# Normalising inside the turn: products with a diagonal instead of transposes, scale and shift on ScalarE, in a hybrid decoder layer

## The chip, the cores and the metric

The kernel runs on one core of a Trainium2 chip. The metric is the device time of one execution in microseconds (us). Five engines work beside each other, each through its own queue in order: TensorE (PE in the profile) multiplies matrices from SBUF into PSUM, VectorE (DVE), ScalarE (ACT) and GpSimd (POOL) work on elements, and SyncE (SP) issues the DMAs.

## The reference, cut to what matters

One layer over x of 512 tokens by 2048 channels, float32: a norm with modulation from the conditioning vector c, a mixing block of sixteen heads (HGRN2 and gated delta rule), a second norm with modulation, and a squared-ReLU MLP of 8192 channels.

```python
def rmsnorm(x, w):
    y = x * lax.rsqrt(jnp.mean(x * x, axis=-1, keepdims=True) + EPS)
    return y * w
mod = silu(c) @ w_ada + b_ada
sh_m, sc_m, gt_m, sh_f, sc_f, gt_f = jnp.split(mod, 6)
h = rmsnorm(x, pre_mix_norm) * (1.0 + sc_m) + sh_m
proj = h @ w_in
y = concatenate([hgrn2_group(proj), gdn_group(proj)]) @ w_out
x = x + gt_m * rmsnorm(y, post_mix_norm)
h = rmsnorm(x, pre_ffn_norm) * (1.0 + sc_f) + sh_f
y = jnp.square(jax.nn.relu(h @ w_ff1)) @ w_ff2
return x + gt_f * rmsnorm(y, post_ffn_norm)
```

The two lines that begin with `h =` are what the change touches. The mean over channels gives one reciprocal root per token; scale and shift are one number per channel.

## The kernel before, in words

Products with large weights want the activations with channels on the partitions, and x arrives with tokens on them. So each of the 16 slices of 128 channels (`kt`) is turned: four blocks of 128 tokens by 128 channels go through TensorE into one PSUM bank of 128 x 512. Every large product is done in a split form: a float32 value is cut into a high part `H` (type float32r) and the rest `L`, and `mm3` adds three products, H by H, H by L and L by H. Weights are split on the way by `WeightStream._split`: ScalarE casts (`wh`, line 197), VectorE or, for some, GpSimd subtracts (`wl`, line 199).

**The start stage.** `ada_thread` (line 786) loads w_ada in slots and adds up the modulation sums `asum`: the scale half on VectorE (line 440), the shift half by ScalarE and GpSimd (lines 449 and 451) from the second slice on. `x_thread` (line 618) squares x on ScalarE as it arrives, gets the reciprocal root of each token block with `rsqrt_to` (VectorE, then a power on GpSimd), multiplies the identity by it (`dgx`, line 641), and spreads it over all partitions by a product of ones with that diagonal (`prx`) and a copy into R1 (line 626). `mod_thread` (line 826) takes the slices one group after the other (0, 1, then pairs). For each it sums the modulation over partitions on TensorE (`pc`), forms the columns `sc1` and `shm` on VectorE, turns the slice (`x_transposes`, line 822, into the bank `wh`, of which there is one; slice 0 is turned early, into `sg`), and then:

- VectorE multiplies the turned slice by the column `sc1` and by R1 into `ht` (line 858);
- for slices below 4 and odd ones, ScalarE adds the shift into `hH` (line 862), and VectorE makes `hL` (line 863);
- for the other six, ScalarE adds the shift into `ht` (line 866) and casts it to `hH` (line 867), and GpSimd subtracts (line 868).

The start products (`start_unit`, line 665; sixteen output blocks of two heads) use each slice as soon as it is there: partial sums leave PSUM by line 703 (ScalarE, first time) or 705 (VectorE, added).

The order on TensorE, ScalarE and SyncE in this stage is the order in which the program issues, and that is set by `run` (line 876): it holds an estimate of TensorE's time (`clock`, advanced by `mm` and `tp` by a fixed cost for each product), lets the thread that is due by that clock go on, and otherwise issues the next start product from the fill thread. VectorE and GpSimd are ordered by the framework. Fill that is not issued in the stage goes on in the mixing stage behind it.

**The middle.** After the output product `pout` (line 1495) the rows z, still with tokens on partitions, get the first norm and the residual (`residual`, line 1464), their reciprocal root again (`rsm`), a diagonal `dg` and its spread into R (`pre_norm`, line 1477), and are stored to DRAM (line 1483). From line 1516 the 16 slices are transposed (`pm`) through four PSUM banks in turn, VectorE applies scale and R (`h2t`, line 1525), and the split follows: for two of three slices by ScalarE and VectorE (lines 1528 and 1529), for the third by two ScalarE passes and GpSimd (lines 1533 to 1535). `ff1` (line 1562) uses the slices at once (`pf`). Here the framework orders the transposes among the `pf` products.

Of the kernel before, what the change touches and what calls it, by code (L numbers as in the profile page):

```python
# [8 lines left out]
F32 = mybir.dt.float32  # L9
# [3 lines left out]
AF = mybir.ActivationFunctionType  # L13
ALU = mybir.AluOpType

P = 128
# [17 lines left out]
T = 512  # L34
# [201 lines left out]
def hybrid_layer_kernel(  # L236
# [7 lines left out]
    nc = tc.nc  # L244
# [80 lines left out]
    def bank(tag, name):  # L325
        return psx.tile([P, T], F32, tag=tag, name=name, bufs={"pj": PJ, "wg": 5 - PJ}.get(tag, 1))
# [3 lines left out]
    def mm(ps, lhsT, rhs, start=True, stop=True, cost=None):  # L330
        nc.tensor.matmul(ps, lhsT=lhsT, rhs=rhs, start=start, stop=stop)  # L331
        n = 1
        for k in rhs.shape[1:]:
            n *= k
        if rhs.dtype == F32R:
            clock[0] += max(n, 256) / 512 * 0.2135
        else:
            m = lhsT.shape[1]
            clock[0] += max(n, m) / 512 * 0.87 if cost is None else cost

    def tp(ps, in_):
        nc.tensor.transpose(out=ps, in_=in_, identity=ident)
        clock[0] += 0.107
# [6 lines left out]
    ident = const.tile([P, P], F32, name="ident")  # L350
    make_identity(nc, ident)
    ones = const.tile([P, P], F32, name="ones")
# [54 lines left out]
    sc1 = const.tile([P, KT], F32, name="sc1")  # L407
# [203 lines left out]
    junk = sp.tile([P, 1024], BF16, name="junkx")  # L611
    rstd = sp.tile([P, 4], F32, name="rstdx")
    stage = sp.tile([P, 4, T], F32, name="stage")
    R1 = sp.tile([P, T], F32, name="R1")
    xn = [xn4[:, tok, :] for tok in range(4)]
    early = {}

    def x_thread():
        yield "xload", 0
        early[0] = bank("sg", "pt0")  # L620
        pr = bank("sh", "prx")

        def spread(tok, dg):
            ts = slice(tok * P, (tok + 1) * P)
            mm(pr[:, ts], ones, dg)
            nc.vector.tensor_copy(out=R1[:, ts], in_=pr[:, ts])

        for tok in range(4):
            for hf in range(2):
                yield max(0.0, xarr[2 * tok + hf] + 1.0 - clock[0])  # L630
                if hf == 0:
                    tp(early[0][:, tok * P : (tok + 1) * P], xn[tok][:, :P])
                nc.scalar.activation(out=junk, in_=xn4[:, tok, hf * 1024 : (hf + 1) * 1024], func=AF.Square,
                                     accum_out=ssx2[:, hf, tok : tok + 1])
                if hf == 0 and tok > 0:
                    spread(tok - 1, dg)
            nc.vector.tensor_tensor(out=ssx[:, tok : tok + 1], in0=ssx2[:, 0, tok : tok + 1],
                                    in1=ssx2[:, 1, tok : tok + 1], op=ALU.add)
            rsqrt_to(rstd[:, tok : tok + 1], ssx[:, tok : tok + 1], 1.0 / D, EPS)
            dg = sp.tile([P, P], F32, tag="dgx", bufs=2, name=f"dgx{tok}")  # L640
            nc.vector.tensor_scalar(out=dg, in0=ident, scalar1=rstd[:, tok : tok + 1], scalar2=None, op0=ALU.mult)
        ws._split()
        yield 2.5
        spread(3, dg)
        yield 0.35
        tokens.add(("x", 0))

# [173 lines left out]

    def x_transposes(ps, kt):
        for tok in range(4):
            tp(ps[:, tok * P : (tok + 1) * P], xn[tok][:, kt * P : (kt + 1) * P])

    def mod_thread():
        for g, kts in enumerate(GROUPS):
            w = len(kts) * P
            if g > 0:
                next(masking, None)  # L830
            if g == 3:
                late_consts()
            yield "ada", g
            yield 2.0 if g else 0.5
            n = len(kts)
            asc, ash = sums.pop(g)
            pc = sm(f"pc{g}").rearrange("p (k n) -> p k n", n=64)
            nr = 1 if g < NV else 512 // w
            for i in range(n):
                column_sum(pc, i, asc[:, i * P : (i + 1) * P], ones[:, :64])  # L840
                for r in range(nr):
                    column_sum(pc, n + i, ash[:, r * w + i * P : r * w + (i + 1) * P], ones[:, :64],
                               r == 0, r == nr - 1)
            ks = slice(kts[0], kts[0] + n)
            nc.vector.tensor_tensor(out=sc1[:, ks], in0=pc[:, 0:n, 0], in1=b_scm[:, ks], op=ALU.add)
            nc.vector.tensor_tensor(out=sc1[:, ks], in0=sc1[:, ks], in1=w_pm[:, ks], op=ALU.mult)
            nc.vector.tensor_tensor(out=shm[:, ks], in0=pc[:, n : 2 * n, 0], in1=b_shm[:, ks], op=ALU.add)
            if g == 0:
                yield "x", 0
            for kt in kts:  # L850
                if kt in early:
                    ps = early[kt]
                else:
                    yield 0.5
                    ps = sm(f"pt{kt}")
                    x_transposes(ps, kt)
                ht = mt("ht", f"ht{kt}", 2)
                nc.vector.scalar_tensor_tensor(out=ht, in0=ps, scalar=sc1[:, kt : kt + 1], in1=R1,
                                               op0=ALU.mult, op1=ALU.mult)
                yield 0.0  # L860
                if kt < 4 or kt % 2:
                    nc.scalar.activation(out=hH[:, kt, :], in_=ht, func=AF.Identity, bias=shm[:, kt : kt + 1])
                    nc.vector.scalar_tensor_tensor(out=hL[:, kt, :], in0=ht, scalar=shm[:, kt : kt + 1],
                                                   in1=hH[:, kt, :].bitcast(F32), op0=ALU.add, op1=ALU.subtract)
                else:
                    nc.scalar.activation(out=ht, in_=ht, func=AF.Identity, bias=shm[:, kt : kt + 1])
                    nc.scalar.copy(out=hH[:, kt, :], in_=ht)
                    nc.gpsimd.tensor_tensor(out=hL[:, kt, :], in0=ht, in1=hH[:, kt, :].bitcast(F32),
                                            op=ALU.subtract)
                yield 1.0  # L870
                tokens.add(("mod", kt))
        yield from decay_terms()
# [572 lines left out]
    with ExitStack() as st:  # L1445
# [4 lines left out]
        ssm = mp.tile([P, 2, 4], F32, name="ssm")  # L1450
        rsm = mp.tile([P, 2, 4], F32, name="rsm")
        junk = mp.tile([P, 1024], BF16, name="junkm")
        R = mp.tile([P, T], F32, name="R")

        def scaled(ps, tok, nb):
            nc.scalar.activation(out=junk[:, :512], in_=ps, func=AF.Square, accum_out=ssy[:, tok, nb : nb + 1])
# [18 lines left out]
            rsqrt_to(rsm[:, 1, tok : tok + 1], ssm[:, 1, tok : tok + 1], 1.0 / D, EPS)  # L1475

        def pre_norm(tok):
            dg = mp.tile([P, P], F32, tag="dg", name=f"dg{tok}", bufs=2)
            nc.vector.tensor_scalar(out=dg, in0=ident, scalar1=rsm[:, 1, tok : tok + 1], scalar2=None, op0=ALU.mult)
            pr = bank("wh", f"pr{tok}")  # L1480
            nc.tensor.matmul(pr[:, :P], lhsT=ones, rhs=dg, start=True, stop=True)
            nc.vector.tensor_copy(out=R[:, tok * P : (tok + 1) * P], in_=pr[:, :P])
            nc.sync.dma_start(out=x2d[tok * P : (tok + 1) * P, :], in_=z[:, tok, :])

        for tok in range(3):
# [30 lines left out]
        for kt in range(KT):  # L1516
            ps = bank(("wg", "wg", "sh", "sg")[kt % 4], f"pm{kt}")
            for tok in range(4):
                nc.tensor.transpose(out=ps[:, tok * P : (tok + 1) * P], in_=z[:, tok, kt * P : (kt + 1) * P],
                                    identity=ident)  # L1520
            if kt == 0:
                h2H = big.tile([P, KT, T], F32R, tag="hH", name="h2H")
                h2L = big.tile([P, KT, T], F32R, tag="hL", name="h2L")
            ht = mp.tile([P, T], F32, tag="ht2", bufs=2, name=f"h2t{kt}")
            nc.vector.scalar_tensor_tensor(out=ht, in0=ps, scalar=sc1f[:, kt : kt + 1], in1=R,
                                           op0=ALU.mult, op1=ALU.mult)
            if kt % 3 < 2:
                nc.scalar.activation(out=h2H[:, kt, :], in_=ht, func=AF.Identity, bias=shf[:, kt : kt + 1])
                nc.vector.scalar_tensor_tensor(out=h2L[:, kt, :], in0=ht, scalar=shf[:, kt : kt + 1],
                                               in1=h2H[:, kt, :].bitcast(F32), op0=ALU.add, op1=ALU.subtract)  # L1530
            else:
                hs = mp.tile([P, T], F32, tag="h2s", bufs=1, name=f"h2s{kt}")
                nc.scalar.activation(out=hs, in_=ht, func=AF.Identity, bias=shf[:, kt : kt + 1])
                nc.scalar.copy(out=h2H[:, kt, :], in_=hs)
                nc.gpsimd.tensor_tensor(out=h2L[:, kt, :], in0=hs, in1=h2H[:, kt, :].bitcast(F32),
                                        op=ALU.subtract)

    partst.close()

# [264 lines left out]
```

## Time and profile before

| | |
|---|---|
| median of 3 runs | 2586.42 us (2584.91 to 2587.82) |
| the profiled execution, its own time | 2583.66 us |
| its span in the trace | 2581.9 us |
| granted TensorE clock, mean | 0.986 |
| TensorE busy | 2469.1 us, 96% |
| VectorE busy | 1875.9 us, 73% |
| ScalarE busy | 1118.1 us, 43% |
| GpSimd busy | 1032.4 us, 40% |

How to read it. The profile is of one execution. Its rows name the line of the kernel, the engine, the operation and the tiles (out <- in), then a count and durations; "L331 PE MATMUL pt<-..." is a product issued by the helper at line 331 into the tile pt. A float32 product shows as two instructions, a transpose as one. Matmul durations overlap, so what a product costs in a stream is the distance between starts. Idle time is put down to what ended it: "<-DVE ht L858" means that VectorE's `ht` came last. The granted clock is TensorE's, as a share of full speed.

### The profile page before, as it was taken

To read this page: it belongs to the slowest core of one execution; us is meant where nothing else is said; L and a number is where in the kernel's file an instruction comes from. 1 tells how busy PE (TensorE), PEld (TensorE's weight loads), DVE (VectorE), ACT (ScalarE), POOL (GpSimd) and SP (SyncE) were. 2 spreads that over 40 slices of the span, in tenths; PEclk is the share of its full clock that TensorE was granted. 3 is DMA by queue.
4 is the path that set the end of the run, shared out by engine and by line. 5 is a ranking of instruction groups with operands and counts; after the bars stand their busy time and mean duration, and the time that the engine had idled before them with its cause. 6 is when DMAs were issued, how large, how long until landed. Compare 5 with 4: busy or idle time off the path is not lost.

```text
span 2581.9 us, 34110 instructions
## 1 busy us (share of the span) xinstructions
PE 2469.1 (96%) x12627; PEld 2007.2 (78%) x12627; DVE 1875.9 (73%) x2709; ACT 1118.1 (43%) x1765; POOL 1032.4 (40%) x646
## 2 busy tenths in 40 slices
PE   5889999998999899999999999999999999999998
PEld 3667777777777778788788888888888888888876
DVE  7997877768586765634668776777768777677787
ACT  5553544544444452423444444444434434443333
POOL 5561344445444440000244535445354444533333
PEclk9999999999999999999999999999999999999999
DMA  8762434444545432344423332433424333232334
GB/s 320 255 203 74 128 119 147 139 148 138 160 142 164 139 115 82 130 140 155 154 98 133 104 135 95 146 123 106 142 95 139 110 127 135 94 114 82 122 116 161
DMA packets 127300, 350.64 MB, mean 136 GB/s; under 512 B 14247, under 2 KB 18713, under 8 KB 125981
## 3 DMA queue, kind: packets, MB, share of 16 engines
q1 hardware_dynamic: 126938, 348.41, 40.0%
q8 instruction: 99, 1.62, 0.3%
q14 instruction: 67, 0.55, 0.1%
q10 hardware_dynamic: 196, 0.06, 0.0%
HBM read 340.01 MB, written 8.40 MB: 135 GB/s over the span
## 4 chain that ended last, share of the span: by engine, by line
PE 67%; DVE 6%; POOL 1%; ACT 1%; issue 1%; DMA 1%; DVEq 0%; ACTq 0%; POOLq 0%
PE pf L331 27%; PE pg L331 22%; PE pj L331 9%; PE pout L331 7%; DVE wl L199 1%; DVE uc L1034 1%; PE pa L331 1%; DVE utmp L1032 1%; POOL y L1728 0%; POOL aacc L451 0%; PE p L331 0%; DVE x2r L1746 0%; DMA ada<-in_w_ada_dram 0%; DVE zkT L493 0%; PE pz L331 0%
## 5 line engine op out<-in xcount | busy, mean ns | idle before, releaser
L199 DVE TENSOR_TENSOR wl<-raw,wh 128x1024 fp32r<-128x1024 f32 x506 | 720.1, 1424 | 427.8 <-ACT wh L197 422.6
L197 ACT CAST wh<-raw 128x1024 fp32r<-128x1024 f32 x512 | 538.0, 1052 | 943.4 <-PE pf L331 285.9
L165 POOL TENSOR_TENSOR raw<-raw,raw 128x1024 f32<-128x1024 f32 x150 | 438.9, 2941 | 392.7 <-DMA raw<-in_w_ff_dram 181.6
L331 PE MATMUL pf<-h2L,wh 128*128 128x512 f32 x1024 | 399.9, 391 | 0.0
L331 PE MATMUL pf<-h2H,wh 128*128 128x512 f32 x1024 | 399.7, 390 | 0.0
L331 PE MATMUL pf<-h2H,wl 128*128 128x512 f32 x1024 | 399.6, 390 | 0.0
L451 POOL TENSOR_TENSOR aacc<-ada,aacc 128x512 f32<-128x512 f32 x180 | 268.9, 1494 | 253.5 <-ACT ada L449 242.2
L331 PE MATMUL pg<-wl,cH 128*128 128x512 f32 x840 | 327.6, 390 | 1.1 <-DVE wl L199 1.1
L331 PE MATMUL pg<-wh,cL 128*128 128x512 f32 x840 | 327.3, 390 | 0.0
L331 PE MATMUL pg<-wh,cH 128*128 128x512 f32 x840 | 327.3, 390 | 0.0
L331 PE MATMUL pj<-hH,wh 128*128 128x512 f32 x768 | 325.2, 423 | 0.0
L331 PE MATMUL pj<-hH,wl 128*128 128x512 f32 x768 | 305.0, 397 | 4.4 <-DVE wl L199 4.4
L331 PE MATMUL pj<-hL,wh 128*128 128x512 f32 x768 | 304.0, 396 | 0.0
L331 PEld LDWEIGHTS pf<-h2H,wh 128*128 128x128 f32 x1024 | 192.7, 188 | 39.7
L331 PEld LDWEIGHTS pf<-h2L,wh 128*128 128x128 f32 x1024 | 192.7, 188 | 39.6
L331 PEld LDWEIGHTS pf<-h2H,wl 128*128 128x128 f32 x1024 | 192.7, 188 | 39.6
L451 POOL TENSOR_TENSOR gacc<-ada,gacc 128x512 f32<-128x512 f32 x64 | 108.4, 1694 | 278.9 <-ACT ada L449 278.9
L1627 DVE TENSOR_TENSOR y<-pg,y 128x512 f32<-128x512 f32 x344 | 219.0, 682 | 0.0
L331 PEld LDWEIGHTS pg<-wl,cH 128*128 128x128 f32 x840 | 157.8, 188 | 35.0 <-DVE wl L199 2.3
L331 PEld LDWEIGHTS pg<-wh,cH 128*128 128x128 f32 x840 | 157.8, 188 | 32.7
L331 PEld LDWEIGHTS pg<-wh,cL 128*128 128x128 f32 x840 | 157.8, 188 | 32.5
L331 PEld LDWEIGHTS pj<-hH,wl 128*128 128x128 f32 x768 | 146.4, 191 | 39.2 <-DVE wl L199 6.5
(434 smaller groups left out, 3770.3 us busy)
## 6 DMA issues: line engine op xcount, KB each, us to landing
raw<-in_w_ff_dram SPq DMA_DIRECT2D x256, 512.0 KB, 4.0
raw<-in_w_in_dram SPq DMA_DIRECT2D x128, 512.0 KB, 3.4
ada<-in_w_ada_dram SPq DMA_DIRECT2D x256, 256.0 KB, 3.4
adas<-in_w_ada_dram SPq DMA_DIRECT2D x128, 256.0 KB, 4.4
raw<-in_w_out_dram SPq DMA_DIRECT2D x40, 512.0 KB, 3.5
xo<-in_x_dram SPq DMA_DIRECT2D x8, 512.0 KB, 9.4
xr<-in_x_dram SPq DMA_DIRECT2D x8, 512.0 KB, 6.8
x2d<-z SPq DMA_DIRECT2D x4, 1024.0 KB, 5.7
```

The source lines that it names most:

```text
L165: self.nc.gpsimd.tensor_tensor(out=out, in0=ra, in1=rb, op=op)
L197: self.cast = self.nc.scalar.copy(out=h, in_=raw).ins
L199: eng.tensor_tensor(out=lo, in0=raw, in1=h.bitcast(F32), op=ALU.subtract)
L331: nc.tensor.matmul(ps, lhsT=lhsT, rhs=rhs, start=start, stop=stop)
L451: nc.gpsimd.tensor_tensor(out=acc, in0=a, in1=acc, op=ALU.add)
L1032: nc.vector.tensor_tensor(out=tmp[:, :, :n], in0=xj, in1=uc[:, :, j : j + 1].broadcast_to([P, NCH, n]), op=ALU.mult)
L1034: nc.vector.tensor_tensor(out=uc[:, :, j + 1 :], in0=uc[:, :, j + 1 :], in1=tmp[:, :, :n], op=ALU.subtract)
L1627: nc.vector.tensor_tensor(out=dst, in0=ps, in1=dst, op=ALU.add)
```

## The change

At both norms the reciprocal root is no longer spread over partitions and multiplied in by VectorE. The turn itself does it: the block of x or z is multiplied by the diagonal `dg` of its tokens' roots instead of by the identity, as an ordinary float32 product. The copies R1 and R, and the products that filled them, go; the four diagonals of each norm are kept. Scale and shift are then applied by ScalarE in one activation from PSUM, twice for each slice in the start stage: once into `hH` and once, in full float32, into `ht`, and `hL` is the difference. In the middle the second, full one (`hs`) is made by VectorE from PSUM for even slices and by ScalarE for odd ones; GpSimd subtracts for every fourth slice, VectorE for the others.

```diff
     def x_thread():
         yield "xload", 0
         early[0] = bank("sg", "pt0")
-        pr = bank("sh", "prx")
-
-        def spread(tok, dg):
-            ts = slice(tok * P, (tok + 1) * P)
-            mm(pr[:, ts], ones, dg)
-            nc.vector.tensor_copy(out=R1[:, ts], in_=pr[:, ts])
...
+    def turn(ps, tok, kt):
+
+        mm(ps[:, tok * P : (tok + 1) * P], xn[tok][:, kt * P : (kt + 1) * P], dgs[tok])
...
                 if hf == 0 and tok > 0:
-                    spread(tok - 1, dg)
+                    turn(early[0], tok - 1, 0)
...
                 ht = mt("ht", f"ht{kt}", 2)
-                nc.vector.scalar_tensor_tensor(out=ht, in0=ps, scalar=sc1[:, kt : kt + 1], in1=R1,
-                                               op0=ALU.mult, op1=ALU.mult)
+                sb = dict(scale=sc1[:, kt : kt + 1], bias=shm[:, kt : kt + 1])
+                nc.scalar.activation(out=hH[:, kt, :], in_=ps, func=AF.Identity, **sb)
+                nc.scalar.activation(out=ht, in_=ps, func=AF.Identity, **sb)
                 yield 0.0
-                if kt < 4 or kt % 2:
-                    nc.scalar.activation(out=hH[:, kt, :], in_=ht, func=AF.Identity, bias=shm[:, kt : kt + 1])
-                    nc.vector.scalar_tensor_tensor(out=hL[:, kt, :], in0=ht, scalar=shm[:, kt : kt + 1],
-                                                   in1=hH[:, kt, :].bitcast(F32), op0=ALU.add, op1=ALU.subtract)
-                else:
-                    nc.scalar.activation(out=ht, in_=ht, func=AF.Identity, bias=shm[:, kt : kt + 1])
-                    nc.scalar.copy(out=hH[:, kt, :], in_=ht)
-                    nc.gpsimd.tensor_tensor(out=hL[:, kt, :], in0=ht, in1=hH[:, kt, :].bitcast(F32),
-                                            op=ALU.subtract)
+                eng = nc.vector if kt < 4 or kt % 2 else nc.gpsimd
+                eng.tensor_tensor(out=hL[:, kt, :], in0=ht, in1=hH[:, kt, :].bitcast(F32), op=ALU.subtract)
                 yield 1.0
...
-            pr = bank("wh", f"pr{tok}")
-            nc.tensor.matmul(pr[:, :P], lhsT=ones, rhs=dg, start=True, stop=True)
-            nc.vector.tensor_copy(out=R[:, tok * P : (tok + 1) * P], in_=pr[:, :P])
+            dg2.append(dg)
...
-                nc.tensor.transpose(out=ps[:, tok * P : (tok + 1) * P], in_=z[:, tok, kt * P : (kt + 1) * P],
-                                    identity=ident)
+                nc.tensor.matmul(ps[:, tok * P : (tok + 1) * P], lhsT=z[:, tok, kt * P : (kt + 1) * P],
+                                 rhs=dg2[tok], start=True, stop=True)
...
+            hs = mp.tile([P, T], F32, tag="h2s", bufs=3, name=f"h2s{kt}")
+            sb = dict(scale=sc1f[:, kt : kt + 1], bias=shf[:, kt : kt + 1])
+            nc.scalar.activation(out=h2H[:, kt, :], in_=ps, func=AF.Identity, **sb)
+            if kt % 2 == 0:
+                nc.vector.tensor_scalar(out=hs, in0=ps, scalar1=sb["scale"], scalar2=sb["bias"],
+                                        op0=ALU.mult, op1=ALU.add)
             else:
...
+                nc.scalar.activation(out=hs, in_=ps, func=AF.Identity, **sb)
+            eng = nc.gpsimd if kt % 4 == 3 else nc.vector
+            eng.tensor_tensor(out=h2L[:, kt, :], in0=hs, in1=h2H[:, kt, :].bitcast(F32), op=ALU.subtract)
```

The early transposes of slice 0 in `x_thread` go too (its turn takes their place), `dgx` and `dg` get four buffers instead of two, and the `ht2` tiles of the middle go.

More of the change, by code (lines that the diff above doesn't have):

```diff
@@ L613, in hybrid_layer_kernel @@
     stage = sp.tile([P, 4, T], F32, name="stage")
-    R1 = sp.tile([P, T], F32, name="R1")
+    dgs = []
     xn = [xn4[:, tok, :] for tok in range(4)]
     early = {}
+    def turn(ps, tok, kt):
+        mm(ps[:, tok * P : (tok + 1) * P], xn[tok][:, kt * P : (kt + 1) * P], dgs[tok])
     def x_thread():
@@ L630, in x_thread @@
                 yield max(0.0, xarr[2 * tok + hf] + 1.0 - clock[0])
-                if hf == 0:
-                    tp(early[0][:, tok * P : (tok + 1) * P], xn[tok][:, :P])
                 nc.scalar.activation(out=junk, in_=xn4[:, tok, hf * 1024 : (hf + 1) * 1024], func=AF.Square,
@@ L639, in x_thread @@
             rsqrt_to(rstd[:, tok : tok + 1], ssx[:, tok : tok + 1], 1.0 / D, EPS)
-            dg = sp.tile([P, P], F32, tag="dgx", bufs=2, name=f"dgx{tok}")
+            dg = sp.tile([P, P], F32, tag="dgx", bufs=4, name=f"dgx{tok}")
             nc.vector.tensor_scalar(out=dg, in0=ident, scalar1=rstd[:, tok : tok + 1], scalar2=None, op0=ALU.mult)
+            dgs.append(dg)
         ws._split()
         yield 2.5
-        spread(3, dg)
+        turn(early[0], 3, 0)
         yield 0.35
@@ L823, in x_transposes @@
         for tok in range(4):
-            tp(ps[:, tok * P : (tok + 1) * P], xn[tok][:, kt * P : (kt + 1) * P])
+            turn(ps, tok, kt)
     def mod_thread():
@@ L1452, in hybrid_layer_kernel @@
         junk = mp.tile([P, 1024], BF16, name="junkm")
-        R = mp.tile([P, T], F32, name="R")
+        dg2 = []
         def scaled(ps, tok, nb):
@@ L1477, in pre_norm @@
         def pre_norm(tok):
-            dg = mp.tile([P, P], F32, tag="dg", name=f"dg{tok}", bufs=2)
+            dg = mp.tile([P, P], F32, tag="dg", name=f"dg{tok}", bufs=4)
             nc.vector.tensor_scalar(out=dg, in0=ident, scalar1=rsm[:, 1, tok : tok + 1], scalar2=None, op0=ALU.mult)
-            pr = bank("wh", f"pr{tok}")
-            nc.tensor.matmul(pr[:, :P], lhsT=ones, rhs=dg, start=True, stop=True)
-            nc.vector.tensor_copy(out=R[:, tok * P : (tok + 1) * P], in_=pr[:, :P])
+            dg2.append(dg)
             nc.sync.dma_start(out=x2d[tok * P : (tok + 1) * P, :], in_=z[:, tok, :])
@@ L1523, in hybrid_layer_kernel @@
                 h2L = big.tile([P, KT, T], F32R, tag="hL", name="h2L")
[L1524 to L1530, printed above, removed]
-            else:
[L1532 to L1536, printed above, removed]
+            hs = mp.tile([P, T], F32, tag="h2s", bufs=3, name=f"h2s{kt}")
[4 more added lines that the diff above has]
+                                        op0=ALU.mult, op1=ALU.add)
+            else:
+                nc.scalar.activation(out=hs, in_=ps, func=AF.Identity, **sb)
+            eng = nc.gpsimd if kt % 4 == 3 else nc.vector
+            eng.tensor_tensor(out=h2L[:, kt, :], in0=hs, in1=h2H[:, kt, :].bitcast(F32), op=ALU.subtract)
     partst.close()
```

## The prediction

> **What bounds the kernel now.** I read the page first, then busy times by stretch, who waited for whom, the tiles that the change touches, and the order of time around line 1516.
>
> ```profile
> span 2581.9 us, 34110 instructions
> PE 2469.1 (96%) x12627; PEld 2007.2 (78%) x12627; DVE 1875.9 (73%) x2709; ACT 1118.1 (43%) x1765; POOL 1032.4 (40%) x646
> PE   5889999998999899999999999999999999999998
> ```
>
> TensorE sets the time: it is busy for 96% of the span, and after the first slices (64.5 us each) nearly always. What adds TensorE work adds time, unless it lands where TensorE now waits. So I look for its gaps, where the change works.
>
> ```profile
> 27.43:60.00 32.57, 24.75 (x110) 18.91 (x112) 30.28 (x46) 19.15 (x43) 14.32 (x10) 0.84 0.85 299
> 60.00:90.00 30.00, 25.53 (x149) 19.73 (x144) 27.15 (x42) 17.94 (x38) 16.37 (x11) 0.94 0.82 298
> 90.00:120.00 30.00, 21.27 (x108) 15.80 (x109) 29.35 (x41) 12.34 (x24) 18.57 (x13) 0.96 0.66 224
> 120.00:150.00 30.00, 26.91 (x125) 20.92 (x124) 26.92 (x36) 15.81 (x31) 18.49 (x13) 0.87 0.75 249
> 150.00:180.00 30.00, 24.94 (x142) 19.37 (x141) 28.30 (x42) 12.58 (x24) 15.13 (x10) 0.89 0.74 237
> 180.00:205.00 25.00, 24.08 (x130) 17.55 (x130) 19.95 (x20) 11.70 (x21) 14.30 (x9) 1.00 0.22 69
> 205.00:230.00 25.00, 25.00 (x117) 19.50 (x116) 12.26 (x21) 12.71 (x24) 3.16 (x5) 1.00 0.21 69
> 1235.50:1246.00 10.50, 4.42 (x28) 3.33 (x26) 6.46 (x15) 3.84 (x8) 1.15 (x3) 0.75 0.44 181
> 1246.00:1270.00 24.00, 24.00 (x119) 19.97 (x118) 21.85 (x27) 15.02 (x23) 6.57 (x5) 0.90 0.10 26
> ```
>
> The columns are the stretch, its length, the busy time of TensorE (PE), its weight loads, VectorE (DVE), ScalarE (ACT) and GpSimd (POOL), then granted clock and DMA. Between 27.43 and 205 TensorE is idle for 7.8 + 4.5 + 8.7 + 3.1 + 5.1 + 0.9 = 30.1 us. VectorE is the full engine there: 111.72 of the 120 us from 60 to 180. From 205 TensorE is full. In the middle it is idle for some 6 us before 1246, then full while the second norm's slices are made.
>
> ```profile
> PE pc L331 <- DVE asum L440: 10.3, 4, 5.9
> PE pt L342 <- DVE shm L847: 4.7, 4, 2.0
> PE pph L331 <- DVE parth L705: 3.7, 1, 3.7
> ...
> ACT ht L866 <- DVE ht L858: 35.6, 6, 9.7
> ACT hH L862 <- DVE ht L858: 16.1, 7, 8.6
> ```
>
> Total wait, times, longest. TensorE waits for VectorE, and ScalarE stood for 51.7 us behind `ht`, the very pass that goes.
>
> **Start stage, the product.** A transpose of a 512-wide slice is four TensorE instructions; a product with a float32 diagonal shows two instructions for each 128x128 block.
>
> ```profile
> 1228.43 0.22 PE pr L1481 x2
> ...
> 1242.87 0.30 DVE dg L1479
> ...
> 1243.21 0.81 PE pr L1481 x2
> ...
> 1244.04 0.30 DVE R L1482
> ...
> 1244.37 0.76 DVE h2t L1525
> ...
> 1254.30 0.44 PE pm L1519 x4
> ```
>
> At full clock one such product, `pr`, advanced TensorE by 0.22 us; four transposes took 0.44. Four products take 4 x 0.22 = 0.88, so a slice costs 0.44 more. Slice 0's blocks and the removed `prx` products lie before 27.43, in idle time. The other fifteen: 15 x 0.44 = +6.6 us. Does the 30 us of idle time hide it? Start products still run long after the stage:
>
> ```profile
> L331 PE MATMUL pph<-hH,wh x112: 388/390/797, 48.8 to 292.1; 128*128 128x512 f32 x112
> ```
>
> `run` (line 876) fills TensorE's order with such products whenever no thread is due on its own clock, and `mm` puts 0.87 us on that clock for a slice where `tp` put 0.43. The longer turn therefore pushes fill out of the stage, to behind 205, where TensorE is full. I count all 6.6 us; what can shrink is the idle time, by itself:
>
> ```profile
> L858 DVE SCALAR_TENSOR_TENSOR ht<-pt,sc,R x16: 739/750/753, 25.9 to 199.6; 128x512 f32<-128x512 f32 x16
> L862 ACT ACTIVATE hH<-ht,shm x10: 706/722/726, 26.7 to 200.4; 128x512 fp32r<-128x512 f32 x10
> L863 DVE SCALAR_TENSOR_TENSOR hL<-ht,shm,hH x10: 744/956/2876, 28.3 to 201.1; 128x512 fp32r<-128x512 f32 x10
> L866 ACT ACTIVATE ht<-ht,shm x6: 722/724/727, 84.0 to 197.9; 128x512 f32<-128x512 f32 x6
> L867 ACT CAST hH<-ht x6: 617/621/624, 84.7 to 198.7; 128x512 fp32r<-128x512 f32 x6
> ...
> L626 DVE COPY R<-prx x4: 292/292/292, 18.1 to 25.5; 128x128 f32<-128x128 f32 x4
> ...
> L705 DVE TENSOR_TENSOR parth<-pph,parth x15: 677/682/692, 78.8 to 232.2; 128x512 f32<-128x512 f32 x15
> ```
>
> **Start stage, VectorE.** It loses 16 x 0.75 = 12.0 us of `ht`, the last copy of R (0.29; the others ran while it waited), and on ten `hL` the difference between 0.744 and a plain subtract, by the nearest row 0.68: 0.6. Together 12.9 us, the upper bound of what the idle time can lose through VectorE. The lower bound is zero, for this reason: `ht` reads PSUM and is never stretched (739 to 753 ns), but `hL`, both inputs in SBUF, went from 744 to 2876. The sums that fill VectorE do the same:
>
> ```profile
> L440 DVE SCALAR_TENSOR_TENSOR asum<-adas,c,asum 128x256 f32<-128x256 f32 x105 | 88.4, 842 | 2.0
> ...
> 152.05 1.00 DVE L440 SCALAR_TENSOR_TENSOR asum<-adas,c,asum 128x256 f32<-128x256 f32 x2
> ```
>
> Two took 1.00 us when undisturbed, so 0.50 each, against a mean of 0.84. GpSimd is busy for 68.6 of the 120 us between 60 and 180, 57%. Freed VectorE time that falls under a GpSimd operation may only become waiting: spread evenly, 43% of 12.9 = 5.5 us would be kept. More was clear of GpSimd, because ScalarE, which feeds it, stood behind `ht`; with that wait gone GpSimd's work will spread over VectorE's. I take 8, between 5.5 and 12.9 and nearer to 5.5.
>
> The Trainium skill, page "SBUF — State Buffer", section "Who interferes with whom", says that a VectorE instruction with two SBUF inputs contends with a GpSimd instruction that reads SBUF, and one with a single SBUF input does not. The trace agrees in those two rows (753 ns at most against 2876). Taken to its end the rule speaks against this change: it takes away only VectorE work that never contended. That is the first rival below.
>
> **Start stage, ScalarE.** Two activations per slice from PSUM with a scale and a bias column replace one of 0.72 (ten slices) or 0.72 + 0.62 (six): 15.3 us now. No row has both columns. Bounds: 0.69, a scale column from PSUM, and 0.79, a column more as between 0.62 and 0.72.
>
> ```profile
> L491 ACT ACTIVATE zkT<-accg,convT 128x512 f32<-128x512 f32 x1 | 0.7, 692 | 0.0
> ```
>
> I take 0.75 for all: 32 x 0.75 = 24 us, 9 more. It costs nothing while the 51.7 us of waiting go; if they did not, ScalarE's 89.5 of 177.6 us between 27.43 and 205 would still leave room. Queued behind ScalarE's new wait, for TensorE's turn in place of VectorE's pass, are the `wh` casts and the `adas` scalings; the wait ends earlier, by VectorE's queue and 0.75.
>
> **The middle, the stream.** From 1246.00 TensorE is full, so a longer turn adds its whole price. Slices 0 to 3 (four banks) are turned before, all but their fourth tokens while TensorE idles, and three of those four blocks fit under the 0.75 us in which ScalarE makes the first `h2H`. The other twelve: 12 x 0.44 = +5.3; the one `pr` that stood in the stream (0.22 at 1228.43) goes: +5.1 us. ScalarE's 24 activations there, 24 x 0.75 = 18 us, and VectorE's eight readings and twelve subtracts, 20 x 0.68 = 13.6, pace nothing: TensorE needs over 24 us for the same slices. A turn now waits for its token's `dg` where a transpose needed only `z`; behind it on TensorE stand only turns and `pf`. The four x2d stores of line 1483 stay where they are.
>
> **The middle, the chain to its first product.**
>
> ```profile
> 1246.00 0.78 PE L331 MATMUL pf<-h2H,wh 128*128 128x512 f32 x1
> ...
> 1247.28 0.78 PE L331 MATMUL pf<-h2L,wh 128*128 128x512 f32 x1
> ```
>
> Now: `dg` ready at 1243.17, `pr` 0.81, R 0.30, `h2t` 0.76, ScalarE 0.72, product at 1246.00. Then: `dg`, the last token's turn for slice 0 (0.81, a product like `pr` at the same low clock), ScalarE 0.75, product at about 1244.9: 1.1 us sooner. For `h2L` of slice 0 VectorE reads the bank that ScalarE reads too. A like pair is ordered in this trace:
>
> ```profile
> 1236.44 0.69 DVE L1457 TENSOR_TENSOR z<-pout,aacc 128x512 f32<-128x512 f32 x1 [0.27 <-ACT junkm L1456]
> ```
>
> VectorE waited for ScalarE's reading of `pout`. So `hs` comes after `h2H` and `h2L` after that: 1244.8 + 0.69 + 0.68 = 1246.2 instead of 1247.28, again 1.1. The low clock (0.75 before 1246, 0.90 after) may lift sooner as the idle stretch ends sooner: between 0 and 0.7 us, I take 0.2. Chain: -1.3 us.
>
> The Trainium skill, page "PSUM — Partial Sum Buffer", section on bank collisions, says that two engines must not access one bank and partition quadrant at the same time, reads included. The wait of 0.27 us agrees. Were both readings allowed at once, `h2L` would come some 0.7 us sooner and the chain would be worth -2.0.
>
> **Sum.** 6.6 - 8 + 5.1 - 1.3 = +2.4 us. The profiled execution took 2583.66 us, 1.8 more than its span, and would take 2586.1. The median of the three runs is 2586.42, 2.8 above it; moved by the same sum it is 2588.8. The VectorE term carries the doubt: at 12.9, with the chain at -2.0, the sum is -3.2 (2583.2).
>
> **The rivals.**
> First, slower: VectorE's time is not what GpSimd leaves, and the 8 us shrink to nothing. For it: asum's 842 ns against 500, and GpSimd's 57%. Against: TensorE's waits name VectorE, and `ht` ran mostly while GpSimd stood. Sum 6.6 + 5.1 - 1.3 = +10.4, 2596.8. It decides, as slower by more than can be told, once less than 5.2 us of VectorE's time are kept. Chance 0.24.
>
> Second, slower, a new wait: slices in a pair share the single `wh` bank, and the odd turn must wait for both of ScalarE's readings.
>
> ```profile
> 130.02 0.60 PE L342 MATMUL pt<-ident,xo 128*128 128x128 f32 x4
> 132.53 0.60 PE L342 MATMUL pt<-ident,xo 128*128 128x128 f32 x4
> ```
>
> From start to start 2.51 us, of which nothing is waiting; with the turn's 0.44 more, 2.95. The turn and two activations need 0.88 + 1.5 = 2.4. If a cast of about 1 us stands before them in ScalarE's queue, 0.5 us is missing in each of seven pairs: +3.5, 2592.3. Against: ScalarE mostly waits there now. Chance 0.08.
>
> Third, faster: the 30.1 us of idle time come from engines waiting in a ring, and with ScalarE out of it half of them go, 15 rather than 8: -4.6, and with the better chain -5.3, 2581.1. Chance 0.15.
>
> **How the numbers follow.** The forecast, VectorE's term between about 5 and 13, has 0.53. A measurement of this kernel can tell about 0.2%, 5.2 us, from no change. The forecast's own range, 2583 to 2592, lies nearly all within it; the first two rivals lie above; the third lies at the edge below, and I count it as faster. Faster 0.15, same 0.53, slower 0.32. The range takes in the first rival's full price and the third's: 2580 to 2597.
>
> **What would show it.** Right: the start stage's last slice (`pt`, last at 199.6 for `ht`) turned 6 to 10 us earlier, start products running to about 290 still, TensorE's idle time between 27 and 205 near 22; ScalarE's waits for `ht` gone; a turn at 0.88 against 0.44; the first `pf` about 1.1 us sooner after `dg`, and the 1246 stretch about 5 us longer. Wrong: four turns in the stream at 0.44 or far above 0.88; asum's mean rising from 842 by more than 70 ns (105 x 0.07 = 7.4 us: VectorE's gift eaten); TensorE waiting for ScalarE at the odd turns; or the stage's end not moving at all.

## The result, and the profile after

| | before | after |
|---|---|---|
| median | 2587.12 us (2584.91 to 2588.05) | 2598.12 us (2597.16 to 2600.45) |
| ratio | | 1.0047, interval 1.0034 to 1.0060 |
| span of the profiled execution | 2581.9 us | 2596.3 us |

The kernel became slower by 11.0 us, where 2.4 us were forecast; the time lies 1 us above the top of the range, next to the first rival's 2596.8.

The page of the kernel after, its span and its engines:

```profile
span 2596.3 us, 34318 instructions
PE 2482.1 (96%) x12739; PEld 2020.5 (78%) x12739; DVE 1858.8 (72%) x2678; ACT 1128.8 (43%) x1778; POOL 1032.2 (40%) x645
```

TensorE has 13 us more work and VectorE 17 us less: the edit did what it says. Where the time came in is read from tiles that mark the ends of stages, first of before, then of after: the first product of the decay terms (`pab`, which needs the last slice, so it marks the end of the start stage), the last start product (`pph`) and the first and last output product (`pout`).

```profile
L331 PE MATMUL pab<-hH,abw x16: 387/397/405, 200.8 to 207.8; 128*32 128x512 f32 x16
L331 PE MATMUL pout<-wh,oH x256: 388/390/507, 1051.7 to 1234.8; 128*128 128x512 f32 x128
```

```profile
L331 PE MATMUL pab<-hH,abw x16: 388/388/414, 203.1 to 210.0; 128*32 128x512 f32 x16
L331 PE MATMUL pph<-hH,wl x112: 388/389/628, 48.9 to 304.1; 128*128 128x512 f32 x112
L331 PE MATMUL pout<-wh,oH x256: 388/389/502, 1062.9 to 1245.6; 128*128 128x512 f32 x128
```

The columns are shortest, median and longest duration in ns, then the first and last start. The start stage ends 2.3 us later, the last start product 11.6 (it was at 292.5), the output product 10.8 to 11.2. Of the 14.4 us between the two spans some 11 come from the start and 3.6 from behind `pout`, in the middle.

Busy time between 27.43 and 205, before and after (TensorE, weight loads, VectorE, ScalarE, GpSimd):

```profile
27.43:205.00 177.57, 147.47 (x751) 112.28 (x752) 161.95 (x223) 89.52 (x178) 97.18 (x64) 0.91 0.69 235
```

```profile
27.43:205.00 177.57, 145.24 (x757) 112.99 (x758) 146.37 (x197) 93.97 (x184) 97.99 (x64) 0.90 0.67 228
```

VectorE is free for 15.6 us more, and TensorE is not idle for 22 us, as forecast, but for 32.3 (30.1 before). So VectorE's freed time became waiting. Who waits in this stretch of the kernel after, TensorE, VectorE and ScalarE in turn (total, times, longest):

```profile
PE pph L331 <- DVE parth L701: 9.6, 2, 6.9
PE pt L331 <- DVE sc L842: 6.3, 3, 2.8
PE pt L331 <- DVE shm L843: 4.5, 2, 2.5
```

```profile
DVE hL L859 <- ACT ht L856: 13.3, 5, 5.9
```

```profile
ACT hH L855 <- PE pt L331: 51.1, 13, 7.1
```

TensorE still waits for VectorE. VectorE waits 13.3 us for the new `ht`. ScalarE's 51.7 us behind VectorE's `ht` have become 51.1 behind TensorE's turn: the wait changed its name and kept its size. Of what the turn itself stood behind, these rows name 10.8 us of waiting for the columns `sc` and `shm`, which are formed from the sums. ScalarE isn't named in TensorE's waits before a turn, so the second rival's new wait didn't come.

The prices of the new operations in the start stage of after:

```profile
L855 ACT ACTIVATE hH<-pt,shm,sc x16: 762/779/781, 25.5 to 201.6; 128x512 fp32r<-128x512 f32 x16
L856 ACT ACTIVATE ht<-pt,shm,sc x16: 764/771/777, 26.1 to 202.3; 128x512 f32<-128x512 f32 x16
L859 DVE TENSOR_TENSOR hL<-ht,hH x10: 680/693/1787, 27.6 to 203.1; 128x512 fp32r<-128x512 f32 x10
```

And its group of sums (busy time, mean ns of one, idle time before them):

```profile
L440 DVE SCALAR_TENSOR_TENSOR asum<-adas,c,asum 128x256 f32<-128x256 f32 x105 | 89.4, 851 | 2.3
```

The activation with two columns takes 0.77 to 0.78 us (estimate 0.75, upper bound 0.79). The subtract is 0.69 where nothing disturbs it. The sums, 851 ns against 842, are as stretched as they were.

The middle, in the order of time, on VectorE and TensorE:

```profile
1253.61 0.28 DVE L1469 TENSOR_SCALAR dg<-ident,rsm 128x128 f32<-128x128 f32 x1 [0.66 <-POOL rsm L427]
...
1253.95 2.08 PE L1507 MATMUL pm<-dg,z 128*128 128x128 f32 x8 [4.49 <-DVE dg L1469]
...
1255.60 0.81 DVE L1516 TENSOR_SCALAR h2s<-pm,sc1f,shf 128x512 f32<-128x512 f32 x1 [1.70 <-ACT h2H L1514]
...
1255.68 0.77 PE L331 MATMUL pf<-h2H,wh 128*128 128x512 f32 x1
...
1259.84 3.73 PE L1507 MATMUL pm<-dg,z 128*128 128x128 f32 x32
```

From `dg` ready to the first `pf` 1.79 us pass (2.83 before): 1.04 sooner, forecast 1.1. VectorE's `h2s` waited for ScalarE's `h2H` on the same bank, as forecast. Four slices turn in 3.73 us, 0.93 each, forecast 0.88. One thing was not foreseen: the framework put two slices of turns (16 instructions from 1256.46) ahead of the first product with `h2L`, which came at 1259.29, 5.40 us after `dg` was ready (4.11 before). TensorE was busy meanwhile, so no idle time came of it. The forecast of the middle held; that of the start did not.

### The profile page after: what moved, and what is told of

Same layout as the page of the kernel before. It is cut to its first block, busy times and chain, and to the rows that moved or that the text cites. A ratio compares the mean times of both kernels' runs of the same rounds, so it can differ in the third digit from the quotient of the medians.

```text
span 2596.3 us, 34318 instructions
## 1 busy us (share of the span) xinstructions
PE 2482.1 (96%) x12739; PEld 2020.5 (78%) x12739; DVE 1858.8 (72%) x2678; ACT 1128.8 (43%) x1778; POOL 1032.2 (40%) x645
## 4 chain that ended last, share of the span: by engine, by line
PE 68%; DVE 5%; POOL 1%; ACT 1%; issue 1%; DMA 1%; DVEq 0%; SPq 0%; ACTq 0%; POOLq 0%
PE pf L331 27%; PE pg L331 22%; PE pj L331 9%; PE pout L331 7%; DVE wl L199 1%; PE pa L331 1%; PE pm L1507 1%; POOL y L1713 0%; DMA ada<-in_w_ada_dram 0%; DVE uc L1024 0%; POOL aacc L451 0%; DVE utmp L1022 0%; PE p L331 0%; DVE x2r L1731 0%; DVE zkT L493 0%
## 5 line engine op out<-in xcount | busy, mean ns | idle before, releaser
L331 PEld LDWEIGHTS pf<-h2L,wh 128*128 128x128 f32 x1024 | 192.2, 188 | 39.8
L331 PEld LDWEIGHTS pf<-h2H,wl 128*128 128x128 f32 x1024 | 192.2, 188 | 39.8
```

## The experiments

My theory after the result: the loss lies in the start, since the turn's price is paid there in full or more, and VectorE's relief is worth next to nothing because GpSimd's additions set the pace of VectorE's sums (the first rival). The theory against it: the relief is worth its 8 us, and something else in the change takes them back, such as the order of the work. Each time stands beside runs of the kernel before on the same chip: 2586.49 us for the first four, 2585.4 for the next four, 2585.45 for the next two, 2587.01 for the last two.

**The two halves of the change.** One kernel has the change's middle on the start of before, the other the change's start on the middle of before.

> Start stage as before, only the second norm's slices in the changed form. The sum for the middle was +5.1 for the longer products and -1.3 for the chain: +3.8 us; the profiles before and after differ by 3.6 us behind the last output product. Every theory of the start stage expects about +3.6 here; if the change's 11 us came mostly from the middle, +8 or more.

> Only the first norm's slices in the changed form, the middle as before. By the two profiles the last output product starts 10.8 us later, so +8 to +11 us here, and with the run before it the two parts add up to the whole. Ring of waits: VectorE's busy time falls by some 15 us between 27 and 205 and its waiting grows by as much. GpSimd in the way: its busy time falls little.

The middle alone: 2589.19 us, ratio 1.0011 (1.0002 to 1.0020), +2.7. The start alone: 2595.81, 1.0035 (1.0023 to 1.0048), +9.3. They add up to 12.0 against 11.0 for the whole. The middle was forecast at 3.8, the start at -1.4: the miss is in the start. In the run with the start alone VectorE's busy time between 27.43 and 205 fell by 12.4 us (161.95 to 149.60), which is nearer to the sign named for a ring of waits than to that for GpSimd in the way.

**The start's two terms apart.** The price alone: before, with the turn made a product with the identity and VectorE's pass kept.

```diff
-            tp(ps[:, tok * P : (tok + 1) * P], xn[tok][:, kt * P : (kt + 1) * P])
+            mm(ps[:, tok * P : (tok + 1) * P], xn[tok][:, kt * P : (kt + 1) * P], ident)
```

> The kernel before with the fifteen later slices of the start turned by a plain product with the identity in place of a transpose: TensorE's longer turn alone, VectorE's pass kept. If the relief of VectorE is worth nothing (ring of waits, or GpSimd), this alone gives most of the start's loss: +6 to +11 us. If the relief is worth its 8 us and the turn costs far more than 6.6, it is +15 us or more.

The relief alone: the changed start, with `turn(ps, tok, kt)` in `x_transposes` put back to the transpose.

> The changed start with the fifteen later slices turned by transposes again: scale and shift on ScalarE and no pass on VectorE, without the longer turn. It leaves out the norm's factor in those fifteen slices; slice 0 keeps it. Relief worth nothing (ring of waits, or GpSimd): -2 to +4 us. Relief worth its 8 us: -6 to -10 us. Ring: VectorE's wait for ScalarE's ht is there as in the changed kernel, 8 us or more. GpSimd: the mean of the asum sums rises by over 70 ns.

Price: 2599.07 us, 1.0047 (1.0034 to 1.0059), +12.6. Relief: 2584.92, 0.9991 (0.9982 to 1.0000), -1.6. Both terms are wrong by themselves: 12.6 for 6.6, and -1.6 for -8. The price lies above the 6 to 11 expected by the theory of a worthless relief, and under the 15 of the other. The relief's time is as that theory expected, but neither of the two signs named with it came: VectorE's wait for ScalarE's `ht` was 2.8 us, not 8 or more, and the sums' mean 851 ns, up by 9 and not by over 70. In the relief run VectorE is busy for 9.2 us less between 27.43 and 205 (152.80, the third busy time), and the stage ends 0.9 us sooner:

```profile
27.43:205.00 177.57, 148.36 (x754) 113.20 (x755) 152.80 (x205) 97.22 (x188) 97.36 (x64) 0.91 0.69 239
```

```profile
L331 PE MATMUL pab<-hH,abw x16: 387/396/417, 199.9 to 206.9; 128*32 128x512 f32 x16
```

Where did the rest go? The sums have two halves, and a slice's columns need both: the scale half on VectorE (line 440) and the shift half, scaled by ScalarE and added by GpSimd (line 451). Their first and last starts, in the kernel before and then in the relief run:

```profile
L440 DVE SCALAR_TENSOR_TENSOR asum<-adas,c,asum x150: 337/484/2593, 5.6 to 193.9; 128x256 f32<-128x256 f32 x105, 128x128 f32<-128x128 f32 x45
L451 POOL TENSOR_TENSOR asum<-adas,asum x52: 1262/1398/2251, 28.6 to 192.2; 128x512 f32<-128x512 f32 x52
```

```profile
L440 DVE SCALAR_TENSOR_TENSOR asum<-adas,c,asum x150: 336/484/2602, 5.6 to 187.7; 128x256 f32<-128x256 f32 x105, 128x128 f32<-128x128 f32 x45
L451 POOL TENSOR_TENSOR asum<-adas,asum x52: 1261/1384/2165, 29.2 to 191.5; 128x512 f32<-128x512 f32 x52
```

VectorE's last sum starts 6.2 us sooner, GpSimd's last addition only 0.7, and in the relief run TensorE's sum over partitions for the last pair of slices waits for GpSimd:

```profile
193.66 0.80 PE L331 MATMUL pc<-ones,asum 128*64 128x64 f32 x20 [1.42 <-POOL asum L451]
```

So VectorE's freed time did reach its sums, and the last slices then stood behind the other half, which hardly moved. From 178.75 us to the end of its last addition at 193.61 GpSimd is idle for 1.4 us. This is read for the last pair; no run sped up the shift half alone.

**Is the price that of the written order?** `run` places start products by its own clock. How many `pph` products lie ahead of the end of the stage: in the kernel before, then in the one with the changed start (the number in brackets; the columns are window, length, busy time):

```profile
0.00:200.80 200.80, 53.01 (x204) 0.92 0.73 253
```

```profile
0.00:202.00 202.00, 49.32 (x168) 0.92 0.71 246
```

36 fewer, and three fewer each of `accg` and `acch`: 42 products that now come behind the stage. At 0.22 to 0.23 us each that is 9.2 to 9.8; the last start product came 91.7 us after the end of the stage and now comes 101.0 after it, 9.3 more. The next kernel is the changed start with one line in `turn`, which takes the product's extra price back out of that clock, so that the order is that of before.

```diff
+        clock[0] -= 0.2175 - 0.107
```

> The changed start with the middle as before, and one line that sets the clock of the hand-made order back by the turn's surplus, so that run() counts a turn at 0.107 as it did a transpose, and gives TensorE the same start products between the slices as before. If the 9.3 us by which the start products run longer behind the stage come from that clock (fill pushed out), the last start product ends at 292 to 296 us in place of 303, and the run is 6 to 9 us faster than the changed start: 0 to +3 us against the kernel before. If TensorE's longer turn costs its time wherever it falls, the stage ends 6 us later instead, and the run stays at +6 to +9.

```profile
L331 PE MATMUL pab<-hH,abw x16: 387/397/423, 206.5 to 213.5; 128*32 128x512 f32 x16
L331 PE MATMUL pph<-hH,wl x112: 387/389/628, 48.7 to 298.2; 128*128 128x512 f32 x112
```

2592.77 us, 1.0030 (1.0018 to 1.0042), +7.4. The 9.3 us of displaced products are gone (206.5 to 298.2 is 91.7 again), and the stage ends 5.7 us later instead of 1.2. The price moved from behind the stage into it, as the expectation's second case had it. By the intervals this kernel can't be told from the +9.3 of the start as it is, so the order's clock is not what made this change lose: TensorE's idle time between 27.43 and 205 did not shrink with it (31.7 us, 30.1 before). Beside the relief run, which has the shorter turn and as many start products inside the stage (204 of `pph` in both), the stage ends 6.6 us later (206.5 and 199.9) and the trace is 6.1 us longer (2589.9 and 2583.8): close to the 6.6 forecast for the turn. The medians lie 9.0 apart, each beside its own runs of the kernel before (+7.4 and -1.6).

**Is it the framework's order on VectorE?** The changed start, with VectorE also held to the order of the program.

```diff
-    with tc.manual_schedule(engines={ET.PE, ET.Activation, ET.SP}):
+    with tc.manual_schedule(engines={ET.PE, ET.Activation, ET.DVE, ET.SP}):
```

> The changed start with the middle as before, and VectorE's queue in the start stage in program order in place of the framework's. If the framework's order on VectorE (hL early in the queue, waiting 13.7 us for ScalarE) is what eats the relief, this differs: VectorE's wait for ht falls below 5 us and the run is 3 to 8 us faster than the changed start, so +1 to +6. If the order is not the cause, +8 to +12.

2611.35 us, 1.0101 (1.0087 to 1.0115), +26. A miss on both counts: this other order is far worse, and VectorE's wait for `ht` grew to 19.5 us, from 13.7 in the changed start, instead of falling below 5. It doesn't show that no better order exists.

**GpSimd's additions taken away.** Before, and the relief run, both without GpSimd's 52 additions into the shift sums.

```diff
-        if not first:
+        if not first and add:
```

> The kernel before without GpSimd's 52 additions to asum in the start stage, so the shift's sums lack most of their terms. The base for the next run. If GpSimd's port use paces the stage, asum's mean on VectorE falls from 842 to about 500 and the stage ends 20 us or more earlier. If a ring of waits paces it, the stage ends less than 10 us earlier although VectorE has 40 us less to do.

> The relief without the longer turn (transposes; the norm's factor left out in fifteen slices), and again without GpSimd's 52 additions. Against the run before it: if GpSimd ate the relief, it is worth its 8 to 13 us now. If the ring eats it, it stays at 0 to 3 us, as it was with GpSimd at work (1.6).

2557.53 us, 0.9892 (0.9879 to 0.9906), -27.9; with the relief 2553.24, 0.9876 (0.9863 to 0.9890), -32.2. In the first, the end of the stage:

```profile
L331 PE MATMUL pab<-hH,abw x16: 387/396/405, 171.6 to 178.6; 128*32 128x512 f32 x16
```

and the group of its sums:

```profile
L440 DVE SCALAR_TENSOR_TENSOR asum<-adas,c,asum 128x256 f32<-128x256 f32 x105 | 61.6, 587 | 2.0
```

The sums fall from 842 to 587 ns and the stage ends 29 us sooner. Between the two kernels the relief is worth 4.3 us, more than the 1.6 with GpSimd at work, and between the two expectations (8 to 13, and 0 to 3). But work was left out, and with it anything that waited for those additions. A kernel that leaves nothing out is the better witness.

**Nothing left out: the sums in PSUM.** VectorE's scale sums are gathered in a PSUM bank and copied out once per group, so that a sum has one operand in SBUF, not two. GpSimd adds as before. The bank comes from a block of start products that now goes through partial sums (its running sum in one more tile).

```diff
-        if i < 5:
+        if i < 4:
             accs[bl] = bank("wg" if i > 2 else "pj", f"acc{nm}")
+        elif i == 4:
+            partial[bl] = oT[:, 15, :]
...
+    asumP = bank("wg", "asumP")
...
-            ada_vector(t[0], w, nr * j, nr, sums[g][0][:, :w], j == 0)
+            accP = asumP[:, g % 2 * 256 : g % 2 * 256 + w]
+            ada_vector(t[0], w, nr * j, nr, accP, j == 0)
...
+                nc.vector.tensor_copy(out=sums[g][0][:, :w], in_=accP)
                 tokens.add(("ada", g))
```

> The kernel before, with nothing left out: VectorE's sums for the scale half are gathered in a PSUM bank instead of in SBUF (so one operand of each sum lies in SBUF, not two) and are copied out once per group; the bank is paid for by the start block (h, 0, C_HF), whose products go through partial sums like those of the blocks after it (8 more adds or copies of some 0.8 us). If the 842 ns of a sum beside GpSimd come of the two engines taking the same SBUF port in turns, a sum falls toward the 0.50 us that it takes while GpSimd is idle, the stage ends 15 to 25 us sooner, and the kernel is 10 to 25 us faster than before. If the sums wait for GpSimd in another way (its additions merely come later), they stay at 0.8 us or over and the time is within 5 us of before, or up to 6 us over it for the added partial sums.

> The same edit on the kernel that has the change's start alone (the 15 products with the diagonals and the scale and shift on ScalarE; the middle as before). If the contention with GpSimd is what kept the start's VectorE relief from paying, then the 0.8 us that the change takes off VectorE in each slice now counts, and this run lies 0 to 6 us over the run above, against 9.3 us between the two without the edit. If the product's own price is what costs, it stays 8 to 13 us over the run above.

On the kernel before: 2558.64 us, 0.9896 (0.9883 to 0.9910), -26.8. On the changed start: 2580.48, 0.9981 (0.9972 to 0.9990). The group of sums in the first of them:

```profile
L440 DVE SCALAR_TENSOR_TENSOR asumP<-adas,c,asumP 128x256 f32<-128x256 f32 x105 | 50.9, 485 | 1.9
```

and the tiles that mark its stages:

```profile
L331 PE MATMUL pab<-hH,abw x16: 387/396/405, 174.7 to 181.7; 128*32 128x512 f32 x16
L331 PE MATMUL pph<-hH,wl x128: 387/389/398, 46.4 to 267.3; 128*128 128x512 f32 x128
```

The same 105 sums take 50.9 us instead of 88.4, with GpSimd adding beside them, and the stage ends 26.1 us sooner, a little more than the theory of the shared SBUF port expected. The runs show that the stretch goes with the second operand in SBUF (the output moved with it here, but `ht`, with its output and one input in SBUF, was never stretched); that a port is what the two engines share, no run shows. The Trainium skill, page "SBUF — State Buffer", section "Who interferes with whom", states it: a VectorE instruction with two SBUF inputs contends with a GpSimd instruction that reads SBUF, since its second input comes through the shared read interface.

The second missed what both theories expected, 21.8 us over the first. Its stage ends even sooner, at 171.1, but the last `pph` comes at 287.1 to 287.5 instead of 267.3. Its busy time by stretch, and the order on SyncE's queue:

```profile
175.00:210.00 35.00, 32.69 (x141) 25.00 (x139) 13.89 (x23) 11.62 (x21) 3.00 (x5) 0.95 0.01 1
210.00:240.00 30.00, 21.43 (x126) 16.71 (x126) 21.13 (x37) 10.80 (x22) 2.31 (x4) 0.83 0.33 114
```

```profile
171.85 0.33 SPq L140 DMA_DIRECT2D raw<-in_w_in_dram  x1
188.73 0.33 SPq L758 DMA_DIRECT2D gd<-gT  x1
209.55 0.38 SPq L962 DMA_DIRECT2D E<-gd  x1
210.04 30.69 SPq L140 DMA_DIRECT2D raw<-in_w_in_dram  x7
```

The last column of the first view is GB/s: 1 between 175 and 210. The displaced products' weights stand in SyncE's queue behind two small transfers of the decay terms, which wait for VectorE (the second, `E`, for 18.0 us until a partial sum of a start product, `xo`, is done); the loads go on at 210, and TensorE is idle for 8.6 us of the next 30. That read as the clock line's doing, which the last pair tests: the same kernel with the clock put back as above, and that one with plain transposes.

> The start changed, the scale half's sums in PSUM, and the written order's own clock put back by what the products add to it, so that the same start products stand inside the stage as in the kernel before with PSUM sums (2558.6 us; the same without the clock put back was 2580.5). If the 22 us between those two are start products that the longer-reckoned turns pushed behind the stage, and the hole that the loads behind them leave there, most of them come back: 2557 to 2568. If they are the products' own time on TensorE, which has no idle time left in this stage, it stays at 2572 or over.

> The same as the run above with plain transposes in place of the products with the diagonals in 15 of the 16 slices (their part of the first norm's factor is left out): VectorE's relief alone, with no contention on its sums and no dearer turn. If the relief is worth something once GpSimd no longer stretches the sums, it lies 2 to 8 us under the kernel before with PSUM sums (2558.6), as the pair without GpSimd's additions did (4.3 us apart). If it is still worth nothing, within 2 us. The run above less this one is the price of the 60 dearer turns where TensorE is nearly full: 60 times 0.11 us, 6.6, if nothing hides it and nothing is added.

The whole start change: 2559.12 us, 0.9893 (0.9876 to 0.9909). The relief alone: 2554.65, 0.9876 (0.9861 to 0.9890). The busy time in the first of them, from 27 to 205:

```profile
27.00:205.00 178.00, 171.06 (x928) 135.43 (x929) 127.56 (x242) 111.62 (x215) 96.34 (x69) 1.00 0.70 243
```

and the tiles that mark its stages:

```profile
L331 PE MATMUL pab<-hH,abw x16: 387/396/422, 174.8 to 181.8; 128*32 128x512 f32 x16
L331 PE MATMUL pph<-hH,wl x128: 388/389/398, 46.9 to 267.4; 128*128 128x512 f32 x128
```

One line of a scheduler's clock is worth 21 us here (2580.48 to 2559.12). From the end of the stage to the end of the last start product, without that line and then with it:

```profile
171.10:287.90 116.80, 105.88 (x624) 82.14 (x625) 79.77 (x169) 41.44 (x84) 8.74 (x14) 0.94 0.22 76
```

```profile
174.80:267.80 93.00, 91.82 (x582) 71.55 (x583) 73.55 (x163) 40.14 (x84) 8.27 (x13) 1.00 0.25 85
```

42 TensorE instructions fewer (the number in brackets), 1.2 us of idle time instead of 10.9 (the length less the first busy time), and a granted clock of 1.00 instead of 0.94: the displaced products and the hole together. With the line, the start change costs nothing and brings nothing: 0.9893 against 0.9896, the same `pab` and `pph` to 0.1 us. Its two terms are there and cancel: the relief 0.0020 of the time, 5 us, the price 4.5 (2559.12 less 2554.65). The intervals overlap by a little, but the runs of the last two kernels don't (2558.41 at least, 2555.74 at most), and the stage's end agrees, 170.8 in the second against 174.7 and 174.8. Against the kernel before with PSUM sums, the relief alone brings VectorE's last sum from 161.4 to 156.2 and GpSimd's last addition from 166.7 to 162.3. TensorE is idle for 7 of the 178 us. By these times the start change doesn't beat PSUM sums alone; no kernel that leaves nothing out is faster, beyond the noise, than the kernel before with the sums in PSUM, 1.0% under the kernel before and 1.5% under the one after (0.9896 by 1.0047).

## Why the prediction was wrong

**The step that failed** is the relief term, "I take 8, between 5.5 and 12.9 and nearer to 5.5". Alone it measured 1.6, beside the price 3.3 (2599.07 less 2595.81). I shared out VectorE's freed time by how much of it GpSimd covers, and let the rest count as time won for the stage. The runs show something else in its place. Most of the freed time was not covered: in the relief run VectorE's busy time fell by 9.2 of the 12.9 us, the sums took 851 ns (842 before), and VectorE's last sum started 6.2 us sooner. But the columns need the shift half too, and GpSimd's last addition came only 0.7 sooner, and the end of the stage 0.9. The text had said of ScalarE's queue, where the scalings for that half stand, that "the wait ends earlier, by VectorE's queue and 0.75"; in the changed kernel it went from 51.7 to 51.1 us, and GpSimd's wait for these scalings from 43.5 to 43.4. What holds the shift half back is open: no run sped it up and left the rest as it was. It does not run by itself, since with VectorE's sums in PSUM its last addition came sooner too (166.7, before 192.2).

**The first rival** was right in size (relief of nothing, 2596.8), and the contention it names is real: without it the stage ends 26 us sooner. That the contention ate the relief is shown only in part. With it gone the relief moved the shift half as well (4.4 us sooner, the stage's end 3.9) and was worth 4 to 5, still not 8. TensorE was then idle for only 13.6 us between 27 and 205 (30.1 before), which leaves less to win.

**The price, +6.6,** was right to be counted in full: idle time didn't hide the turn, and the clock pushed products out, as the text said. Its size held where the order was kept: 6.6 us at the end of the stage and 6.1 between the spans (the run with the clock put back against the relief run), 4.5 without the contention. What the term left out is what the pushed-out products do: 6.6 us on that clock pushed out 42 products, 9.3 us, and the stage ended later as well, +12.6 alone and +10.9 beside the relief (2595.81 less 2584.92).

**The middle, +5.1 and -1.3,** held: 3.8 forecast, 3.6 between the traces, 2.7 (0.5 to 5.2) alone. The chain to the first product came 1.04 us sooner for 1.1, and the bank's order was as the trace of before had shown it. The chain to `h2L` ended in no earlier product, and the 0.2 for the clock was not measured by itself.

**ScalarE,** 9 us more and off the path, held in price (0.775 for 0.75). The condition "while the 51.7 us of waiting go" did not come true: they became 51.1 behind the turn. In the changed kernel VectorE waited 13.3 us for ScalarE's second activation, which the text didn't name; where that wait was 2.8 us, in the relief run, the relief was still worth only 1.6.

**Of what would show it wrong,** one came true in substance: the end of the stage didn't come sooner but 2.3 us later. Another came in part: in the changed start alone the sums rose to 880 ns, 38 more where the text had named 70 (105 times 38 ns, 4 us of the gift eaten); in the whole change, with the same start, they rose by 9, so the larger rise isn't the rule.

**The chances:** slower had 0.32, the first rival 0.24. The forecast's 8 rested on a guess, for which the text showed no row, on how GpSimd's work would spread once ScalarE was free.

## What to carry to other kernels

Before counting what an engine will save, look at what else the waiting step needs: here the sums had a second half on other engines, and 6.2 us won on the first half moved the end of the stage by 0.9. Look also at whether the engine's other instructions are stretched (one form, shortest against mean): here taking away 9.2 us of unstretched work bought 1.6 us, while moving one operand of the stretched work to PSUM bought 26.8. A price put on an order written by an estimated clock moves other work too: compare how many fill products lie ahead of the end of the stage, and what their loads queue behind, before calling the price the instruction's own. And a wait that goes is only a gain if its waiter's next input is early; ScalarE's 51.7 us changed their name and stayed.

## What was not expected of the hardware

VectorE's 128x256 sum, reading and writing its running sum in PSUM, took 485 ns, no more than the 0.50 us of two SBUF inputs left undisturbed. A VectorE pass from PSUM with two columns took 0.81 us for 128x512, against 0.69 for the subtract; the prediction had 0.68 to 0.69 for both.

```profile
L1516 DVE TENSOR_SCALAR h2s<-pm,sc1f,shf x8: 805/810/812, 1255.6 to 1270.1; 128x512 f32<-128x512 f32 x8
L1521 DVE TENSOR_TENSOR h2L<-h2s,h2H x12: 684/691/693, 1256.4 to 1270.9; 128x512 fp32r<-128x512 f32 x12
```
